# The last wait of a one-core kernel: from SyncE's queue to GpSimd's

## The chip, the cores and the metric

The kernel runs on one core of one Trainium2 chip. The metric is the device time of one execution in microseconds (us). The profile comes from one profiled execution. In it, "SPq" is the queue of SyncE (SP), "POOLq" that of GpSimd (POOL); DVE is VectorE, ACT is ScalarE, PE is TensorE. Semaphore instructions and instructions that issue DMAs are not counted as busy time.

## The reference

The kernel computes, for x of 32 x 512 x 1024 float32, the sum over the last axis of max(x, 0):

```python
relu_x = np.maximum(x, 0)
return np.sum(relu_x, axis=-1).astype(np.float32)
```

The input is 67.11 MB, the result 32 x 512 float32, 0.07 MB.

## The kernel before

The 16384 rows are dealt to 128 partitions. Seven blocks of 16 rows a partition are loaded by SyncE into three buffers of SBUF in turn (`io0` to `io2`, `load`, line 106); from the fourth on, a load waits until VectorE has freed its buffer. Blocks are clamped in place by ScalarE (`clamp`, line 147) and summed by VectorE (`total`, line 155). Single rows of some blocks go another way: GpSimd takes two rows of the sixth block (`pool_rows`, lines 205 and 211), and ScalarE and VectorE take the seventh block row by row with an accumulator (`act_row`, line 162, and `dve_row`, line 170). The last 16 rows come in smaller and smaller loads (`TAIL`, then four rows in pieces of columns), so that little is left to do when the last one has landed. GpSimd clamps one small piece there (line 278). TensorE multiplies a piece of a buffer eight times (`multiply`, line 188); nobody reads its result.

There is no scheduler: each engine's stream is in the order in which the lines are written, and all waits are written out by hand on semaphores that the kernel allocates itself (`Semaphores`).

The sums lie in the tile `res`. SyncE stores them in three pieces (`store`, line 118): the first 16 columns, the middle 110, and the last two. Each store raises the semaphore `stored` by 16 when it has landed. The last store waits for the last two sums, one by VectorE (line 299) and one by ScalarE (line 124).

Behind these streams stands a last block, whose own instructions the kernel throws away and replaces by two: `sem_clear` (line 52) sets all semaphores but `stored` back to zero, and line 53 waits until `stored` has reached 16 for each of the three stores, 48 in all, and takes the 48 off again, so that every semaphore of the kernel is at zero for the next execution. `open_without_barrier` (called in line 54) then removes the barrier at the start and moves the first load into the opening block.

The order of SyncE's queue at the end is thus: the last loads, store 1, store 2, store 3, a branch to the last block, line 52, line 53. GpSimd's ends with line 278 and a branch to the last block, which holds nothing for it.

## Time and profile before

| | |
|---|---|
| median of three runs | 160.99 us (160.98 to 161.06) |
| the profiled execution | 160.82 us |
| its span, first to last instruction | 159.5 us |
| VectorE busy | 118.8 us (74%) |
| ScalarE busy | 101.5 us (64%) |
| GpSimd busy | 12.6 us (8%) |
| HBM read and written | 67.11 and 0.07 MB, 421 GB/s over the span |

The span goes from the first to the last instruction that the program itself holds. The time of an execution also covers something outside it, 160.82 - 159.5 = 1.3 us in the profiled one. Part 6 of the page lists the issues of DMAs with their time to landing; these are the stores:

```profile
out_dram<-res SPq DMA_DIRECT2D x1, 55.0 KB, 1.6
out_dram<-res SPq DMA_DIRECT2D x1, 8.0 KB, 31.0
out_dram<-res SPq DMA_DIRECT2D x1, 1.0 KB, 1.4
```

The columns are: what is written from what, the queue that issues, the number, the size, and the us from issue to landing. The store of 1.0 KB is the last one.

### The profile page before, as it was taken

Reading aid. Unit: us, or ns where it says so; the run is one execution under the profiler, and the core shown is the slowest. Engines: PE = TensorE matmul, PEld = TensorE weight load, DVE = VectorE, ACT = ScalarE, POOL = GpSimd, SP = SyncE. Lnnn points to the kernel's source line nnn. Section 1 sums busy time; section 2 is a strip of 40 time slices with the busy share of each in tenths; the row PEclk is TensorE's granted clock in tenths of the full one; section 3 lists DMA queues with packets and bytes.
Section 4 is the critical chain, followed back from the end, with each engine's and each line's share of the span. In section 5 each row is a group of like instructions: output and inputs, shape, how many; then the busy total and the mean of one; then the engine's idle time right before and its main releaser. Section 6 shows DMA issues by size and latency. Waiting matters only on the chain.

```text
span 159.5 us, 164 instructions
## 1 busy us (share of the span) xinstructions
PE 9.0 (6%) x16; PEld 3.7 (2%) x16; DVE 118.8 (74%) x44; ACT 101.5 (64%) x49; POOL 12.6 (8%) x16
## 2 busy tenths in 40 slices
PE   0000000000000000000000000000000000000696
PEld 0000000000000000000000000000000000000241
DVE  0000000007999799999999999999999799999986
ACT  0000059992699708996099951999329970496995
POOL 0000000000000000000000000000029960000001
DMA  7996996996998999979969969969969989698994
GB/s 279 510 526 263 526 526 263 526 510 279 526 427 362 526 394 394 526 312 477 526 263 526 526 263 526 526 263 526 493 296 526 411 378 526 296 493 366 423 401 141
DMA packets 2304, 67.18 MB, mean 421 GB/s; under 512 B 640, under 2 KB 768, under 8 KB 1024
## 3 DMA queue, kind: packets, MB, share of 16 engines
q1 hardware_dynamic: 2304, 67.18, 98.1%
HBM read 67.11 MB, written 0.07 MB: 421 GB/s over the span
## 4 chain that ended last, share of the span: by engine, by line
DMA 44%; DVE 37%; ACT 13%; PE 6%; SPq 0%; issue 0%
DMA io<-in_x_dram 44%; DVE res L155 31%; ACT io L147 13%; DVE io L170 6%; PE ps L188 6%; SPq L106 0%
## 5 line engine op out<-in xcount | busy, mean ns | idle before, releaser
L155 DVE TENSOR_REDUCE res<-io 128x8 f32<-128x8192 f32 (+2 forms) x10 | 101.1, 10173 | 38.7 <-ACT io L147 38.7
L147 ACT ACTIVATE io<-io 128x8192 f32<-128x8192 f32 (+2 forms) x10 | 81.8, 8218 | 25.9 <-DMA io<-in_x_dram 25.9
L162 ACT ACTIVATE io<-io 128x1024 f32<-128x1024 f32 x16 | 16.7, 1043 | 8.7 <-DMA io<-in_x_dram 8.7
L188 PE MATMUL ps<-io 128*128 128x512 f32 x16 | 9.0, 728 | 149.0 <-DVE io L170 149.0
L170 DVE TENSOR_SCALAR_CACHE_REDUCE io<-io 128x1024 f32<-128x1024 f32 x14 | 16.2, 1215 | 0.5 <-DMA io<-in_x_dram 0.4
L145 ACT ACT_TABLE_LOAD x1 | 1.3, 1283 | 21.8 <-DMA io<-in_x_dram 21.8
L205 POOL TENSOR_SCALAR io<-io 128x2048 f32<-128x2048 f32 x1 | 5.4, 5354 | 118.2 <-DMA io<-in_x_dram 118.2
L188 PEld LDWEIGHTS ps<-io 128*128 128x128 f32 x16 | 3.7, 242 | 153.5 <-DVE io L170 149.0
L211 POOL TENSOR_TENSOR io<-io 128x1024 f32<-128x1024 f32 (+8 forms) x9 | 6.0, 670 | 0.7
L162 ACT ACTIVATION_READ_ACCUMULATOR io<-io 128x1 f32 x16 | 3.0, 186 | 0.0
L278 POOL TENSOR_SCALAR io<-io 128x254 f32<-128x254 f32 x1 | 0.8, 842 | 24.4 <-DMA io<-in_x_dram 24.4
L170 DVE DVE_READ_ACCUMULATOR io<-io 128x1 f32 x14 | 1.2, 83 | 0.0
L129 DVE TENSOR_SCALAR_CACHE_REDUCE io<-io 128x552 f32<-128x552 f32 (+1 forms) x2 | 1.1, 596 | 0.0
L124 ACT ACTIVATE io<-io 128x321 f32<-128x321 f32 (+1 forms) x2 | 0.9, 426 | 0.1
L299 DVE SCALAR_TENSOR_TENSOR io<-last,io 128x254 f32<-128x254 f32 x1 | 0.4, 424 | 0.0
L124 ACT ACTIVATION_READ_ACCUMULATOR io<-io 128x1 f32 x2 | 0.4, 187 | 0.0
L124 ACT ACTIVATE last<-last 128x153 f32<-128x153 f32 x1 | 0.3, 330 | 0.0
L211 POOL TENSOR_TENSOR res<-io 128x2 f32<-128x2 f32 x1 | 0.2, 194 | 0.1
L124 ACT ACTIVATION_READ_ACCUMULATOR last<-last 128x1 f32 x1 | 0.2, 185 | 0.0
L129 DVE DVE_READ_ACCUMULATOR io<-io 128x1 f32 x2 | 0.2, 82 | 0.0
L344 POOL MEMSET const-float32-0.0<- 128x1 f32 x1 | 0.1, 99 | 0.2 <-issue 0.2
L344 POOL MEMSET const-bfloat16-1.0<- 128x1 bf16 x1 | 0.1, 101 | 0.0
(3 smaller groups left out, 0.3 us busy)
## 6 DMA issues: line engine op xcount, KB each, us to landing
io<-in_x_dram SPq DMA_DIRECT2D x1, 4096.0 KB, 23.8
io<-in_x_dram SPq DMA_DIRECT2D x1, 2048.0 KB, 28.3
io<-in_x_dram SPq DMA_DIRECT2D x1, 1151.0 KB, 30.6
io<-in_x_dram SPq DMA_DIRECT2D x1, 436.5 KB, 31.2
io<-in_x_dram SPq DMA_DIRECT2D x1, 259.0 KB, 31.4
last<-in_x_dram SPq DMA_DIRECT2D x1, 201.5 KB, 31.4
io<-in_x_dram SPq DMA_DIRECT2D x7, 29.1
out_dram<-res SPq DMA_DIRECT2D x1, 55.0 KB, 1.6
```

The lines of the kernel that those rows point to most:

```text
L124: nc.scalar.activation(out=ap, in_=ap, func=RELU, accum_out=accum_out).wait_op(*after, "sem-ge").then_inc(sems.end, 1)
L129: i = nc.vector.tensor_scalar(out=ap, in0=ap, scalar1=0.0, scalar2=None, op0=MAX, op1=ADD, accum_out=accum_out,)
L145: nc.scalar.preload_act_table(RELU).wait_op(loaded, 16, "sem-ge")
L147: i = nc.scalar.activation(out=ap, in_=ap, func=RELU)
L155: nc.vector.tensor_reduce(out=res[:, m : m + n], in_=ap, axis=mybir.AxisListType.X, op=ADD).wait_op(sems.act, n_act, "sem-ge").then_inc(se ...
L162: i = nc.scalar.activation(out=ap, in_=ap, func=RELU, accum_out=accum_out)
L170: i = nc.vector.tensor_scalar(out=ap, in0=ap, scalar1=0.0, scalar2=None, op0=MAX, op1=ADD, accum_out=accum_out,)
L188: i = nc.tensor.matmul(ps[:, :], rows_of[:, 0, :P], rows_of[:, 1, :MM_COLS], start=True, stop=True)
L205: i = nc.gpsimd.tensor_scalar(out=ap, in0=ap, scalar1=0.0, scalar2=None, op0=MAX)
L211: nc.gpsimd.tensor_tensor(out=ap[:, :, :w] if w > 1 else res[:, m : m + n].unsqueeze(2), in0=ap[:, :, :w], in1=ap[:, :, w : 2 * w], op=ADD,)
L278: nc.gpsimd.tensor_scalar(out=clamped, in0=clamped, scalar1=0.0, scalar2=None, op0=MAX).wait_op(loaded, 16, "sem-ge").then_inc(sems.end, 1)
L299: nc.vector.scalar_tensor_tensor(out=clamped, in0=last[:, : 2 + LAST_DVE], scalar=0.0, in1=clamped, op0=MAX, op1=ADD, accum_out=res[:, NT ...
```

## The change

GpSimd's queue, in place of SyncE's, gets the instruction that waits for the three stores and takes their 48 off the semaphore. The clear of the other semaphores stays with SyncE, and so do the stores. Each engine's other instructions stay as they were, in their order.

```diff
     cleared = range(nums[0], nums[-1] + 1)
     assert len(cleared) == len(nums)
     nc.sync.sem_clear(cleared)
-    nc.sync.wait_ge(sems.stored, 16 * n_stores).then_inc(sems.stored, -16 * n_stores)
+    nc.gpsimd.wait_ge(sems.stored, 16 * n_stores).then_inc(sems.stored, -16 * n_stores)
     open_without_barrier(tc, EARLY)
```

## The prediction

> **What bounds the kernel now.** I read the page's chain of waits first, then the timeline of the last three microseconds, then the waits of SyncE's own queue, then the single rows of lines 52, 53 and 344, and at the end the semaphore records of the trace. The chain:

> ```profile
> DMA 44%; DVE 37%; ACT 13%; PE 6%; SPq 0%; issue 0%
> DMA io<-in_x_dram 44%; DVE res L155 31%; ACT io L147 13%; DVE io L170 6%; PE ps L188 6%; SPq L106 0%
> ```

> The reader is to see that the 159.5 us of the span are loads, clamps and sums, none of which the change touches. The chain is followed back from the last busy instruction, a matmul that ends at 158.06 us. The last store and the wait for it lie behind that, so they are looked for in the timeline and in SyncE's waits:

> ```profile
> 155.32 0.84 POOL L278 TENSOR_SCALAR io<-io 128x254 f32<-128x254 f32 x1 [24.39 <-DMA io<-in_x_dram]
> ...
> 156.52 1.86 SPq L118 DMA_DIRECT2D out_dram<-res  x2
> ...
> 157.94 0.08 DVE L299 DVE_READ_ACCUMULATOR io<-last,io 128x1 f32 x1
> ```

> ```profile
> SPq L118 <- DVE io L299: 1.2, 1, 1.2
> SPq L53 <- SPq L53: 1.0, 1, 1.0
> ```

> ```profile
> L53 SPq EVENT_SEMAPHORE  x1: 17/17/17, 159.5 to 159.5; - x1
> ```

> ```profile
> L52 SPq EVENT_SEMAPHORE_RANGE_CLEAR  x1: 58/58/58, 158.4 to 158.4; - x1
> ```

> The reader is to see three things. GpSimd's last work of the kernel ends at 155.32 + 0.84 = 156.16 us. The result is complete at 157.94 + 0.08 = 158.02, the last store is issued at 158.05, and SyncE clears its range at 158.43 to 158.49 while that store is in flight. Then SyncE sits in line 53 for 1.0 us, and its row of 17 ns is the last of the span.

> The semaphore records give the finer times (us from the span's start). The stores' semaphore gets its last sixteen increments between 159.280 and 159.452; line 53 starts at 159.469 and takes the count down at 159.486, the end of the span. The profiled execution took 160.82 us, 1.32 us more than the 159.50 of its span; the 160.99 us of the unprofiled runs is 0.17 us above it, so I add the change to both. What fills most of the time behind the span stands in the same records, on semaphore 2, which no line of the kernel names:

> ```
> pass before the kernel    -0.375 -0.340 -0.302 -0.259 -0.235 | -0.123 -0.085 -0.050 -0.004
> pass after the kernel    158.214 158.248 158.286 158.330 159.617 | 159.661 159.699 159.734 159.781
> last pass                160.574 160.608 160.646 160.690 160.714 | 160.811 160.849 160.884 160.930
> single updates of semaphores 7 to 255, in five blocks, between the two last passes: 159.744 to 160.353
> ```

> **The change, part by part.** One instruction moves: the wait for 48 with the decrement, from the end of SyncE's stream to the end of GpSimd's. No DMA moves, no queue has anything behind the instruction but the closing pass, and no load, store, clamp or sum is earlier or later, so the last increment at 159.452 stays.

> On SyncE: it loses 17 ns of row and the 1.0 us of wait. It finishes at 158.49 with the range clear and, leaving as it does now in 0.131 us, would be ready to report at 158.62, well inside the store's flight; this saves nothing by itself, because the pass then stops at GpSimd instead. Without that cover (0.83 us up to 159.45) its own exit would count.

> On GpSimd: the wait starts after 156.16 and is a cover of 3.3 us for whatever precedes it. Four terms follow the last increment.

> First, waking up. SyncE needs 159.469 - 159.452 = 0.017 us. GpSimd's standing wait is in no row; the nearest are two loads that free ScalarE and GpSimd alike, where GpSimd starts 0.05 us later (155.32 against 155.27; the timeline shows the same at 118.57 against 118.52). Bounds 0 and +0.05; those rows also contain the start of arithmetic, so I take +0.02.

> Second, the instruction itself: SyncE's row is 17 ns; GpSimd's nearest row without arithmetic is 27 ns:

> ```profile
> L344 POOLq INC_SWDGE_SEM  x1: 27/27/27, 0.1 to 0.1; - x1
> ```

> I take +0.01, bounds 0 and +0.01.

> Third, the exit, from the kernel's last instruction to the report. SyncE's is 0.131 us. GpSimd's can't be seen, as it is over long before anybody asks. It may be near 0, which is -0.13. From above, the nearest row is the earliest complete pass of the launch, where place 3 reports at -2.731, 1.025 us after place 2 at -3.756: some engine can be a microsecond late in such code, so +0.9. Between these, the nearest like for like is how soon a released engine does its next thing: SyncE's block begins 0.127 us after its release (159.617 to 159.744), the blocks that begin next begin 0.11 to 0.15 after theirs. I take +0.02.

> Fourth, the pass. When SyncE is last, four releases follow: 159.781 - 159.617 = 0.164 us. When a lower place is last, the places above it must still report, and then all are released. The last pass, in which nobody above place 1 is late, has these steps: 0, 34, 72, 116, 140 ns up, and 237, 275, 310, 356 down. From the report of place 4, 3, 2 or 1 to the end that is 240, 284, 322 or 356 ns; against 164 it costs 0.076, 0.120, 0.158 or 0.192 us. Which place is GpSimd's? Before the kernel SyncE's first instruction comes 0.235 us after its release; GpSimd's first, at 0.130, comes 0.253, 0.215, 0.180 or 0.134 after the release of place 4, 3, 2 or 1. Places 4 and 3 fit best, and I take the third: +0.12, bounds +0.076 and +0.192.

> [...]

> Sum: 0.02 + 0.01 + 0.02 + 0.12 = +0.17 us. The profiled execution would go from 160.82 to 160.99, the median from 160.99 to 161.16, 0.1% slower. With the small terms at either bound but the exit kept near SyncE's, the change is +0.06 to +0.30.

> **The rivals.** *GpSimd leaves slowly.* The exit that nobody could see is now on the path. For it speaks that one place was 1.0 us late at launch, that the third place is the one I hold for GpSimd's, and that GpSimd alone opens with rows of configuration at the start of the kernel. Against it: the third place's release-to-work and report-to-report times are like the others' (38 ns a step). The price is up to 0.9 us above SyncE's exit: 160.99 + 0.9 + 0.15 = 162.04; it decides from an exit 0.17 us longer than SyncE's, where the time passes 161.31. Its middle is near 161.6.

> *Not slower: the exit turns out short.* The one mechanism that pays here is that SyncE's 0.131 us of leaving is now done during the store's flight. If GpSimd's own exit takes next to nothing and it sits at place 4, the change is -0.131 + 0.076 + 0.02 = about -0.04 us, 160.95. From place 4 it decides where GpSimd leaves in less than 0.03 us (0.131 - 0.076 - 0.03); from place 3 it needs an exit under 0.01 and a waking that costs nothing more than SyncE's. Against it: no engine is seen to do its next thing in under 0.11 us after a release.

> *The closing pass isn't in the measured time.* Then only the first three terms remain, +0.05 us, 161.04. Against it: 1.32 us lie outside the span, and the pass, the resets and the last pass end 1.44 us after the span, which is close.

> **How the numbers follow.** A measurement of this kernel can tell about 0.2%, 0.32 us, from no change. The forecast, 161.16 with its own range of 161.05 to 161.30, has 0.56; the slow exit 0.33; the short exit 0.06; the pass outside the time 0.05. Slower by over 0.2% (above 161.31) is the slow exit and a little of the forecast's upper edge, 0.35. Faster by over 0.2% (below 160.67) has no mechanism of this size, since at most 0.13 + 0.03 us of SyncE's can be hidden at all: 0.03. Within 0.2% is the remainder, 0.62. The range goes from 160.95, the point of the second rival, to 161.70, which takes in the lower and middle part of the slow exit and leaves out about 0.13 above it; below it perhaps 0.03.

> **What would show it.** In the changed kernel's trace the last row is line 53 on GpSimd's queue, it begins within 0.07 us of the last increment of the stores' semaphore, and SyncE's last row is the range clear near 158.5. On semaphore 2, the reports stop at GpSimd's place until about 0.15 us after the decrement and then run on in 0.28 us. The place where the reports stop settles the fourth term, the gap after the decrement the third. The prediction is wrong if that gap is over 0.3 us, or if the resets behind the pass last longer or shorter than 159.781 to 160.353, or if the loads and stores themselves move.

## The result

The changed kernel took 161.46 us (median of 7 runs, 161.37 to 161.63) against 160.99 (7 runs, 160.89 to 161.33): the ratio is 1.0031, 95% interval 1.0021 to 1.0040, so 0.34 to 0.64 us more. The forecast was +0.17 us. The time lies in the predicted range and on the predicted side, but the difference is about three times the forecast, and it falls where the rival "GpSimd leaves slowly" was put (above 161.31).

The profiled execution took 161.57 us. Part 1 and part 4 of its page have the kernel's work as it was; the first line is part 1 before, the second is part 1 now, and the line of part 4 is the one before to the letter:

```profile
PE 9.0 (6%) x16; PEld 3.7 (2%) x16; DVE 118.8 (74%) x44; ACT 101.5 (64%) x49; POOL 12.6 (8%) x16
```

```profile
PE 9.1 (6%) x16; PEld 3.8 (2%) x16; DVE 118.8 (74%) x44; ACT 101.5 (64%) x49; POOL 12.6 (8%) x16
...
DMA io<-in_x_dram 44%; DVE res L155 31%; ACT io L147 13%; DVE io L170 6%; PE ps L188 6%; SPq L106 0%
```

The span is 159.7 instead of 159.5, and the chain in order of time says where that comes from (columns: start, us, what; the single line is from before, the three from after):

```profile
0.43 40.65 DMA io<-in_x_dram
```

```profile
0.43 40.88 DMA io<-in_x_dram
41.30 0.02 issue
41.33 13.87 ACT io L147
```

The first loads took 40.88 us; before they took 40.65. Everything behind them is later by the same 0.2 us, and that is the loads of one execution, not the change: the spans of the changed kernel's seven runs go from 159.5 to 159.7 us, those of the kernel before, in the 32 runs beside the first experiments, from 159.4 to 159.9. The end of the timeline has the same shape as before, 0.20 to 0.21 later:

```profile
155.53 0.84 POOL L278 TENSOR_SCALAR io<-io 128x254 f32<-128x254 f32 x1 [24.37 <-DMA io<-in_x_dram]
...
156.73 1.85 SPq L118 DMA_DIRECT2D out_dram<-res  x2
...
158.14 0.08 DVE L299 DVE_READ_ACCUMULATOR io<-last,io 128x1 f32 x1
```

The rows of lines 52 and 53 show that the instruction is where the diff put it:

```profile
L52 SPq EVENT_SEMAPHORE_RANGE_CLEAR  x1: 58/58/58, 158.6 to 158.6; - x1
```

```profile
L53 POOLq EVENT_SEMAPHORE  x1: 17/17/17, 159.7 to 159.7; - x1
```

The reader is to see that SyncE's queue now ends with the clear, and that the wait on GpSimd is a row of 17 ns, as on SyncE. So nothing in the span explains half a microsecond. Outside the span there are 161.57 - 159.695 = 1.875 us, instead of 160.82 - 159.486 = 1.334. The trace's records of semaphore 2 show that time (us from the span's start, read as in the prediction, places 1 to 5 reporting and then 4 to 1 released; the row of line 53 ends at 159.486 before and at 159.695 after):

```
before, pass after the kernel   158.214 158.248 158.286 158.330 159.617 | 159.661 159.699 159.734 159.781
after,  pass after the kernel   158.472 158.506 160.261 160.305 160.329 | 160.426 160.466 160.500 160.547
before, last pass               160.574 ... 160.930
after,  last pass               161.336 ... 161.693
```

Places 1 and 2 report at once, and the pass stops at place 3 for 1.75 us. That is GpSimd. From the end of its row to its report pass 160.261 - 159.695 = 0.566 us; SyncE needed 159.617 - 159.486 = 0.131. Then the pass runs on in 160.547 - 160.261 = 0.286 us where SyncE's was followed by 0.164. From the release of place 1 to the end of the last pass it is 1.146 us, before 1.149. The two differences, 0.435 + 0.122 = 0.557 us, account for the 0.54 us by which the time outside the span grew. That is not a matter of one execution: time less span, with spans on record to 0.1 us, is 1.88 us on average in the seven runs of the changed kernel and 1.33 in the 32 of the kernel before, 0.55 us apart.

### The profile page after: what moved, and what is told of

It is laid out like the page before. It is cut to its first block, busy times and chain, and to the rows that moved or that the text cites. A ratio compares the mean times of both kernels' runs of the same rounds, so it can differ in the third digit from the quotient of the medians.

```text
span 159.7 us, 164 instructions
## 1 busy us (share of the span) xinstructions
PE 9.1 (6%) x16; PEld 3.8 (2%) x16; DVE 118.8 (74%) x44; ACT 101.5 (64%) x49; POOL 12.6 (8%) x16
## 4 chain that ended last, share of the span: by engine, by line
DMA 44%; DVE 37%; ACT 13%; PE 6%; SPq 0%; issue 0%
DMA io<-in_x_dram 44%; DVE res L155 31%; ACT io L147 13%; DVE io L170 6%; PE ps L188 6%; SPq L106 0%
## 5 line engine op out<-in xcount | busy, mean ns | idle before, releaser
L155 DVE TENSOR_REDUCE res<-io 128x8 f32<-128x8192 f32 (+2 forms) x10 | 101.1, 10172 | 38.9 <-ACT io L147 38.9
L147 ACT ACTIVATE io<-io 128x8192 f32<-128x8192 f32 (+2 forms) x10 | 81.8, 8218 | 25.9 <-DMA io<-in_x_dram 25.9
L188 PE MATMUL ps<-io 128*128 128x512 f32 x16 | 9.1, 730 | 149.3 <-DVE io L170 149.3
L170 DVE TENSOR_SCALAR_CACHE_REDUCE io<-io 128x1024 f32<-128x1024 f32 x14 | 16.2, 1218 | 0.5 <-DMA io<-in_x_dram 0.4
L188 PEld LDWEIGHTS ps<-io 128*128 128x128 f32 x16 | 3.8, 242 | 153.7 <-DVE io L170 149.3
L278 POOL TENSOR_SCALAR io<-io 128x254 f32<-128x254 f32 x1 | 0.8, 842 | 24.4 <-DMA io<-in_x_dram 24.4
L170 DVE DVE_READ_ACCUMULATOR io<-io 128x1 f32 x14 | 1.2, 87 | 0.0
L299 DVE SCALAR_TENSOR_TENSOR io<-last,io 128x254 f32<-128x254 f32 x1 | 0.4, 425 | 0.0
L344 POOL MEMSET const-float32-0.0<- 128x1 f32 x1 | 0.1, 99 | 0.2 <-issue 0.2
L344 POOL MEMSET const-uint8-127<- 128x1 uint8 x1 | 0.1, 103 | 0.0
```

Source lines behind the costliest of these rows:

```text
L147: i = nc.scalar.activation(out=ap, in_=ap, func=RELU)
L155: nc.vector.tensor_reduce(out=res[:, m : m + n], in_=ap, axis=mybir.AxisListType.X, op=ADD).wait_op(sems.act, n_act, "sem-ge").then_inc(se ...
L170: i = nc.vector.tensor_scalar(out=ap, in0=ap, scalar1=0.0, scalar2=None, op0=MAX, op1=ADD, accum_out=accum_out,)
L188: i = nc.tensor.matmul(ps[:, :], rows_of[:, 0, :P], rows_of[:, 1, :MM_COLS], start=True, stop=True)
L278: nc.gpsimd.tensor_scalar(out=clamped, in0=clamped, scalar1=0.0, scalar2=None, op0=MAX).wait_op(loaded, 16, "sem-ge").then_inc(sems.end, 1)
L299: nc.vector.scalar_tensor_tensor(out=clamped, in0=last[:, : 2 + LAST_DVE], scalar=0.0, in1=clamped, op0=MAX, op1=ADD, accum_out=res[:, NT ...
```

## The experiments

Two questions were open. Is the long way out GpSimd's own, or does any engine but SyncE leave so late when it comes last? And if it is GpSimd's, does it come from the place of the wait, from what GpSimd did in the kernel, or is it always there? In each kernel I read the gap from the end of the waiting row to the report. The kernels go by their labels: wait_scalar, wait_vector, wait_tensor, hidden_exit, hidden_late, late_mm2, nopool_gp, nopool_sp, idle_mm2 and tiny_mm2.

**The wait on the other engines.** One word of line 53 is changed, to `nc.scalar`, `nc.vector` or `nc.tensor`:

```diff
-    nc.gpsimd.wait_ge(sems.stored, 16 * n_stores).then_inc(sems.stored, -16 * n_stores)
+    nc.scalar.wait_ge(sems.stored, 16 * n_stores).then_inc(sems.stored, -16 * n_stores)
```

The trace of the kernel before has, from an engine's last row to the report of the place these theories give it, 158.248 - 158.014 = 0.23 us on ScalarE, 158.330 - 158.022 = 0.31 on VectorE and 158.214 - 158.062 = 0.15 on TensorE; the lower ends of the ranges below are estimates.

> ScalarE takes the final wait. Theory (the length of the way out is GpSimd's own): ScalarE's way out takes 0.10 to 0.23 us and it reports at place 2, from which the pass to the release of place 1 takes 0.32 us against 0.16 with SyncE last: +0.16 plus -0.03 to +0.10, that is 161.12 to 161.25. Rival (any engine other than SyncE that comes last leaves in about 0.56 us): +0.43 + 0.16 = about 161.6.

> VectorE takes the final wait. Theory: its way out takes 0.13 to 0.31 us and it reports at place 4, from which the pass takes 0.24 us against 0.16: +0.08 plus 0 to +0.18, that is 161.07 to 161.25. Rival (any engine other than SyncE): +0.43 + 0.08 = about 161.5.

> TensorE takes the final wait. Theory: its way out takes about 0.15 us and it reports at place 1, from which the whole pass of 0.36 us follows, against 0.16: +0.19 + 0.02 = about 161.2. Rival (any engine other than SyncE): +0.43 + 0.19 = about 161.6.

Their rows of line 53, one from each kernel's trace:

```profile
L53 ACTq EVENT_SEMAPHORE  x1: 17/17/17, 159.7 to 159.7; - x1
```

```profile
L53 DVEq EVENT_SEMAPHORE  x1: 21/21/21, 159.6 to 159.6; - x1
```

```profile
L53 PEldq EVENT_SEMAPHORE  x1: 51/51/51, 159.7 to 159.7; - x1
```

Together with semaphore 2 and the runs (in each, one place is late; "gap" is the end of the row to its report, "pass" its report to the release of place 1; the sum is compared with SyncE's 0.131 + 0.164 = 0.295):

| wait on | place | gap us | pass us | sum less 0.295 | ratio to before, 95% interval | in us |
|---|---|---|---|---|---|---|
| ScalarE | 2 | 0.138 | 0.325 | +0.168 | 1.0015, 1.0006 to 1.0024 | +0.10 to +0.39 |
| VectorE | 4 | 0.188 | 0.242 | +0.135 | 1.0010, 1.0001 to 1.0019 | +0.02 to +0.31 |
| TensorE | 1 | 0.236 | 0.358 | +0.299 | 1.0023, 1.0014 to 1.0032 | +0.23 to +0.51 |
| GpSimd (the change) | 3 | 0.566 | 0.286 | +0.557 | 1.0031, 1.0021 to 1.0040 | +0.34 to +0.64 |

Every sum lies in the interval of its runs. Time less span leaves out the scatter of the loads and says the same more sharply: it averages 1.33 us before, 1.50 with ScalarE, 1.47 with VectorE and 1.61 with TensorE, which is 0.18, 0.15 and 0.29 us more. The medians were 161.16, 161.12 and 161.32 us against 160.94. All four places are now settled, since each time the pass stopped at another one. The rival "any engine but SyncE leaves in 0.56 us" falls: ScalarE leaves in 0.138 us, SyncE in 0.131. TensorE came out above the forecast of 161.2, because its gap is 0.236 instead of 0.15 and its row is 51 ns instead of 17, and its waking takes 0.029 us against SyncE's 0.017.

**The wait on GpSimd, but early.** The second store gets a semaphore of its own, and GpSimd waits for that one; SyncE keeps the other two (hidden_exit; "..." stands for lines left out):

```diff
-    nc.sync.wait_ge(sems.stored, 16 * n_stores).then_inc(sems.stored, -16 * n_stores)
+    nc.gpsimd.wait_ge(sems.second, 16).then_inc(sems.second, -16)
+    nc.sync.wait_ge(sems.stored, 32).then_inc(sems.stored, -32)
...
+        self.second = tc.alloc_semaphore("second")
...
-            sems.stored, 16
+            sems.second if n_store == 1 else sems.stored, 16
```

> GpSimd waits for the second store alone, on a semaphore of that store, and SyncE keeps the wait for the other two, the last one among them. Theory (GpSimd always needs about 0.56 us from its last instruction to its report): the second store lands near 158.1, GpSimd's report on semaphore 2 comes about 0.56 us after its decrement, near 158.7, instead of 158.29, and nothing is lost, since SyncE reports at about 159.6: time as before, 160.99, within 0.1 us. Rival (GpSimd is slow only where its wait is the kernel's last event): its report follows 0.13 to 0.2 us after its decrement, near 158.3; the time is also as before, so the gap is what tells them apart.

The time was 161.02 us against 160.94, ratio 1.0007 (0.9997 to 1.0016): no loss that can be measured. But the gap told nothing. GpSimd's row ended at 158.364, place 1 (TensorE) reported only at 158.959, and place 3 followed it at 159.032, so GpSimd's gap is only known to be at most 0.668. Next, SyncE passed the semaphore on after its clear, to make GpSimd later than TensorE (hidden_late; the lines left out are those of hidden_exit):

```diff
-    nc.sync.wait_ge(sems.stored, 16 * n_stores).then_inc(sems.stored, -16 * n_stores)
+    nc.sync.wait_ge(sems.second, 16).then_inc(sems.second, 1)
+    nc.gpsimd.wait_ge(sems.second, 17).then_inc(sems.second, -17)
+    nc.sync.wait_ge(sems.stored, 32).then_inc(sems.stored, -32)
...
```

> As hidden_exit, but SyncE passes the second store's semaphore on after its range clear, so that GpSimd's wait ends near 158.75, later than TensorE's report (158.2 to 159.0 so far). Theory (GpSimd always needs about 0.56 us from its decrement to its report): the reports stop at place 3 until about 159.3, still ahead of SyncE's at about 159.85; the time stays that of before, 160.94 on the last chip, within 0.1 us. Rival (slow only as the kernel's last event): place 3 reports 0.13 to 0.2 us after GpSimd's decrement or directly behind place 2, near 158.95.

161.01 us against 160.93, ratio 1.0002 (0.9993 to 1.0011), and again no answer: in this execution TensorE reported at 159.481, and place 3 directly behind at 159.554. TensorE's eight multiplications were what covered GpSimd, so the same kernel was run with two of them (`N_MM` from 8 to 2).

> hidden_late again with two of TensorE's eight multiplications instead of eight, so that TensorE reports early and can't cover GpSimd's report (it reported at 159.48 in hidden_late, 0.70 us after GpSimd's decrement, and left that question open). Theory (GpSimd always needs about 0.56 us): places 1 and 2 report before 158.7, place 3 at GpSimd's decrement + 0.56, near 159.3; SyncE's report follows its own decrement by 0.13 as before. Rival (slow only as the last event of the kernel): place 3 at decrement + 0.13 to 0.2, near 158.95.

GpSimd's wait is line 54 of this kernel:

```profile
L54 POOLq EVENT_SEMAPHORE  x1: 17/17/17, 158.8 to 158.8; - x1
```

```
late_mm2, pass after the kernel   153.195 158.353 159.384 159.428 159.855 | 159.899 159.937 159.971 160.018
```

The row starts at 158.800 and ends at 158.817; place 3 reports at 159.384, 0.567 us later, while SyncE's own wait still runs to 159.712. The gap is that of the change within a nanosecond, with GpSimd far from being the last. No loss shows here: the one time is 161.04 us, and before on the same chip, also once, 161.04. So the 0.56 us follow GpSimd's wait even where it is not the kernel's last event, and SyncE's wait then covers them. Whether they also follow where GpSimd's stream ends with arithmetic, as before the change, no run shows: before, its last row ended at 156.16, and place 2, ahead of it, reported only at 158.248.

**GpSimd without work.** GpSimd's two rows of the sixth block go to ScalarE and VectorE, the clamp of line 278 is left out, and the wait stays on GpSimd or on SyncE:

```diff
-TWO = [[16], [16], [8, 8], [8, 8], [8, 8], [7, 7], []]
+TWO = [[16], [16], [8, 8], [8, 8], [8, 8], [8, 8], []]
 ACT = [0, 0, 0, 0, 0, 0, 8]
-POOL = [0, 0, 0, 0, 0, 2, 0]
+POOL = [0, 0, 0, 0, 0, 0, 0]
...
-    nc.gpsimd.tensor_scalar(
-        out=clamped, in0=clamped, scalar1=0.0, scalar2=None, op0=MAX
-    ).wait_op(loaded, 16, "sem-ge").then_inc(sems.end, 1)
...
```

> GpSimd takes the final wait as in the change, and has no arithmetic of its own: its two rows of the sixth block go to ScalarE and VectorE, and the clamp of the 254 columns of the last but one row is left out. Theory A (GpSimd's way out is a fixed stretch of closing code): decrement to report 0.56 us again. Theory B (the way out grows with what the engine was set up for or did, its configuration rows and its arithmetic): 0.15 to 0.25 us. The total moves also by VectorE's and ScalarE's extra work, so it is to be compared with nopool_sp alone: A gives nopool_sp + 0.56, B gives nopool_sp + 0.15 to 0.25.

> The partner of nopool_gp: the same work left out and moved, and SyncE keeps the final wait. SyncE's decrement to report stays at 0.13 us in both theories. Time: before, plus what two more rows cost VectorE and ScalarE in the sixth block, minus GpSimd's, about +1 us or less in both theories.

Both were much slower than the +1 us that was expected, 163.79 and 163.73 us, ratios to before 1.0176 (1.0162 to 1.0190) and 1.0155 (1.0136 to 1.0173), and the difference of 0.56 us between the two did not show: 0.06 in the medians, with the second kernel's runs spread from 163.1 to 164.03. TensorE's timeline of the profiled execution of nopool_gp says why:

```profile
152.07 10.11 PE L188 MATMUL ps<-io 128*128 128x512 f32 x16 [152.07 <-DVE io L170]
```

With VectorE's larger share (103.3 us in line 155 against 101.1 before, and 39.6 us idle ahead of it against 38.7) the multiplications start 3 us later, at 152.07 instead of 149.04, and they end at 162.18, after the last store has landed (161.79). TensorE, place 1, reports at 162.327, and GpSimd, whose row had ended at 161.835, directly behind it. In nopool_sp place 1 reports at 162.637, after SyncE's row had ended at 162.090. In both profiled executions TensorE was the last, so who waits for the stores did not count in them. It was not so in every run: time less span is 1.52 us in the profiled run of nopool_gp but 1.82 to 1.87 in its three others, near the 1.88 of the change. The shortest run of nopool_gp, 163.72 us, lies 0.6 us above the two shortest of nopool_sp, 163.10 and 163.13. Both fit an exit of 0.56 us, but no trace of these runs is there to show it. Two multiplications in place of eight take TensorE's cover away, with GpSimd idle or almost idle:

> nopool_gp again with two of TensorE's eight multiplications: GpSimd has no arithmetic and no configuration rows in the body, its work is moved and in part left out as there, and it takes the final wait. Theory A (a fixed stretch of closing code): decrement to report 0.56 us. Theory B (what the engine was set up for or did): 0.15 to 0.25 us. In nopool_gp the report came at 0.556, but directly behind TensorE's, so that it only bounded it from above.

> idle_mm2 with a memset and one tensor_scalar of 128 x 2 elements on GpSimd at the start of the body, which bring the configuration rows back. Theory A: 0.56 us as in idle_mm2. Theory B, if idle_mm2 is short: 0.56 us here would put it on the configuration, as in idle_mm2 would put it on the amount or the lateness of the arithmetic.

```profile
L53 POOLq EVENT_SEMAPHORE  x1: 17/17/17, 162.0 to 162.0; - x1
```

```profile
L222 POOLq MODIFY_POOL_CONFIG  x2: 11/11/11, 0.4 to 0.4; - x2
L222 POOL TENSOR_SCALAR tiny<-tiny x1: 211/211/211, 0.5 to 0.5; 128x2 f32<-128x2 f32 x1
```

The first row is of idle_mm2, which has no configuration row at all; the other two are of tiny_mm2 and show that the configuration is back there with an almost empty operation. In idle_mm2 the wait ends at 162.004 and place 3 reports at 162.565, a gap of 0.561. In tiny_mm2 it is 161.832 and 162.399, a gap of 0.567. The times, one of each, are 163.89 and 163.72 us, which is 1.89 us more than the span in both, against 1.875 in the change. Neither the arithmetic nor the configuration makes the gap: theory A holds, by one trace of each kernel.

## Why the prediction was partly right

The path was right: the loads, sums and stores did not change, SyncE's way out is hidden (its last row ends at 158.686, and it reports 0.024 us behind place 4) but the pass stops at GpSimd, GpSimd is place 3, and what is lost lies outside the span. The side was right. The size was off, by one term. The range held the time only because it had been widened for the rival: the forecast's own range, 161.05 to 161.30, missed it, and "slower by over 0.2%" had been given a chance of 0.35, against 0.62 for a time within 0.2%.

*The waking* was taken as +0.02 us; the last increment came at 159.654 and the row began at 159.678, 0.024 against SyncE's 0.017, so +0.007.

*The instruction* was taken as +0.01; it is 17 ns on both, so nothing.

*The exit* was taken as +0.02 with bounds of -0.13 and +0.9; it measured 0.566 - 0.131 = +0.435. This is the step that failed, and by the mark that the prediction set (a gap over 0.3 us). I chose the value by the gap between a release and the next reset, 0.11 to 0.15 us on four of the five engines by that reading (0.22 on the fifth). That gap was no measure of the exit: GpSimd reports in step with the others within a pass (38 ns a step) and yet takes four times SyncE's time from its last instruction to its first report. The row that pointed the other way was the launch, where place 3 came in 1.0 us behind place 2; I gave that reading a third of the chance. It is no measure of the exit either: in the twelve traces here that lag goes from 0.5 to 1.4 us.

*The pass* was taken as +0.12; it measured 0.286 - 0.164 = +0.122. With TensorE last, the whole pass took 0.358 us, against 0.356 in the last pass of the kernel before (160.574 to 160.930).

The sum with the measured terms is 0.007 + 0 + 0.435 + 0.122 = 0.564 us instead of 0.17, and the runs say 0.34 to 0.64. The row of the wait is 17 ns on both queues, but the exits are not equal: 0.131 us on SyncE and 0.566 on GpSimd. Two readings of the prediction are off without weight in the sum: with the span of 159.486, 1.33 us lie outside it and not 1.32, and the single updates of semaphores 7 to 255, which the prediction reads as resets, end at 160.349 and not at 160.353.

Of the rivals, the slow exit happened, with about half of its upper price. The short exit is refuted by the gap of 0.566 us. The pass outside the measured time is refuted by ScalarE and TensorE: waking, row and exit alone would cost them +0.01 and +0.15 us, and the intervals begin at +0.10 and +0.23.

What stays open is what GpSimd does in those 0.56 us. The trace has no row in them, and none of the kernels changed them: 0.566, 0.567, 0.561 and 0.567. In all four GpSimd's stream ends with the same kind of instruction, a wait with a decrement, so the runs can't tell a cost of leaving from one of leaving after such a wait. On ScalarE the difference was small: place 2 reported 0.108 us after its last accumulator read in idle_mm2 and 0.138 after the wait in wait_scalar.

## What to carry to other kernels

An engine's way out after its last instruction was part of the time here when that engine came last (0.566 us with GpSimd, 0.131 with SyncE), and it cost nothing that could be seen while another engine was still busy (late_mm2: 0.567 us, and the time that of before, 161.04). For a kernel like this one, let the engine with the shortest exit and the last place in the closing pass (here SyncE, 0.131 + 0.164 us) hold the last wait, and let GpSimd (0.566 + 0.286) and TensorE (0.236 + 0.358) end well before. A cost that the trace hid behind a wait was sized here by what the engines do elsewhere, and came out wrong; when such a cover is taken away, keep both ends of the bound in mind and look for the row nearest to that code. When you measure a hidden gap, first make sure that no third engine covers it, as TensorE did here in hidden_exit, hidden_late and nopool_gp.

## What the runs showed that was not expected

GpSimd needs 0.56 us from its wait, as its last instruction, to its report, with or without work in the kernel, where ScalarE needs 0.138, VectorE 0.188 and TensorE 0.236. The wait takes 51 ns of row on TensorE, against 17 to 21 on the others.

TensorE's end is less steady than the kernel's: with the same eight multiplications, place 1 reported at 158.21, 158.47, 158.57, 158.96 and 159.48 us in five kernels (before, after, wait_vector, hidden_exit, hidden_late). In the last one only 0.35 us were left up to SyncE's own report at 159.83. With two multiplications (late_mm2) it reported at 153.20, and the one time was that of the kernel before.
